# Summing the conditioning products on VectorE alone in a two-layer decoder trunk

## The chip, the cores and the metric

The kernel runs on one core of a Trainium2 chip. The metric is the device time of one execution in microseconds; lower is better. Three runs of the kernel before took 2589.61, 2590.52 and 2591.8 us.

## The reference, cut to what matters

The program is a decoder trunk of two layers on one sequence of 256 tokens, 2048 features wide, all in float32. Each layer norms its input, scales and shifts it by conditioning vectors, multiplies it with a wide input projection, mixes it in four head groups, multiplies the result with an output projection, adds it to the input through a gate, and does the same again around a gated feed-forward part. The conditioning vectors are what the change touches. They come from one vector `c` and a large matrix:

```python
cond = jax.nn.silu(c)
for l in range(DEPTH):
    mod = cond @ w_ada[l] + b_ada[l]
    shift1, scale1, gate1, shift2, scale2, gate2 = [m[:, None, :] for m in jnp.split(mod, 6, axis=-1)]
    h = rms_norm(x, norm1_w[l]) * (1.0 + scale1) + shift1
    mixed = mixer_groups(h, positions, w_in[l], ...)
    x = x + gate1 * (mixed @ w_out[l])
    h = rms_norm(x, norm2_w[l]) * (1.0 + scale2) + shift2
```

`w_ada` has 2048 rows and 12288 columns per layer, 100.7 MB. So each element of it is used once, for one product and one addition.

## The kernel before

**Dense products.** Every weight matrix is cut into pieces of 256 rows and up to 512 columns (512 KB). `prepare` loads a piece into a raw buffer from SyncE's queue (L254), ScalarE rounds it to a first float32r part `whi` (L243), and VectorE subtracts that from the raw piece to get the second part `wlo` (L246). TensorE multiplies both parts with the split activations in three products (L339 to L341, or L376 to L378). There are nine raw buffers, shared with the conditioning pieces, and four of each part; pieces are prepared three ahead. So ScalarE waits for TensorE to free a part, VectorE waits for ScalarE, and TensorE reads what both made.

**Conditioning products.** They are cut into 24 sums: in each layer four `ada_pair` sums for each of two norms (512 columns of a shift and the same 512 of a scale) and two `ada_gate` sums for each of two gates (1024 columns). One sum takes 16 units, one for each 128 rows of the matrix, so there are 384 units. A unit loads 512 KB into a raw buffer (L401 or L403). Then it goes one of two ways, by its number `k` and the tuple `on_pool`. The first unit is written into the accumulator `acc` by VectorE (L406). Units that are not in `on_pool` are multiplied and added into `acc` by one VectorE instruction (L408). Units in `on_pool` are scaled in place by ScalarE (L410) and added into a second accumulator `accb` by GpSimd (L411). `accb` is cleared by GpSimd at the first unit (L394), and the bias lands in its first partition by DMAs from GpSimd's queue (L396). `ODD` has six units (1, 3, ... 11) and serves the first four sums; `HALF` has seven (1, 3, ... 13) and serves the other twenty. That makes 164 units on GpSimd, 196 multiply-adds and 24 first units on VectorE.

**End of a sum.** After the last unit of a deferred sum, GpSimd adds `accb` to `acc` (L431 for a pair, L455 for a gate). Then TensorE sums over the partitions: for a pair by eight small matmuls with a vector of ones (L441), whose result VectorE takes over (L445, L446). The first four sums are not deferred: TensorE does eight matmuls on `accb` and then eight on `acc`, in one PSUM group. A gate's sum is split into two parts and broadcast by TensorE (L470).

**Order of the work.** The order on each engine is the order in which the Python code issues, and each engine works its queue in that order. The units wait in a queue `bg` with a due time counted in weight pieces; after each half block `pump` issues as many of them as the due times ask for, so units stand between the steps of the dense products and of the mixers on every engine. `require` issues what is left of a sum at the point where its result is needed. Accumulators are tiles of a ring of 24, which also holds activations, gates and mixer tiles.

Of the kernel before, what the change touches and what calls it, by code (L numbers as in the profile page):

```python
# [35 lines left out]
LA = 3  # L36
# [44 lines left out]
def decoder(ctx: ExitStack, tc: tile.TileContext, x_d, c_d, pos_d, w_ada, b_ada, n1_d, w_in, w2_d, b2_d,  # L81
            gnw_d, sink_d, lb_d, hnw_d, w_out, n2_d, w_fi, w_fd, fnw_d, cf_d, out_d):
    nc = tc.nc
# [6 lines left out]
    two = ctx.enter_context(tc.tile_pool(name="two", bufs=6))  # L90
# [19 lines left out]
    def MB(shape, n="m"):  # L110
        return mps.tile(shape, F32, tag="m", name=nm(n))
# [4 lines left out]
    V, A, G, TE = nc.vector, nc.scalar, nc.gpsimd, nc.tensor  # L116
# [6 lines left out]
    rows = con.tile([NROWS, P], F32, name="rows")  # L123
# [30 lines left out]
    ones = con.tile([P, 1], F32, name="ones")  # L154
# [11 lines left out]
    cond = con.tile([P, KT], F32, name="cond")  # L166
# [94 lines left out]
    def fill(n=LA):  # L261
        while len(ready) < n and (plan or cur[0] is not None):
            prepare()
# [13 lines left out]
    later = []  # L277
# [102 lines left out]
                    half()  # L380
            pump()

    # ---- conditioning vectors: products with silu(c) summed over rows on VectorE, or on ScalarE and GpSimd,
    # then over partitions on TensorE
    def ada(l, c0, pair, on_pool, finish, defer, dl):
        st = {}
        w = 512 if pair else 1024
        np_ = 1024 // w

        def unit(k):  # L390
            if k == 0:
                st["a"] = T4([P, np_, w], n="acc")
                st["b"] = T4([P, np_, w], n="accb")
                G.memset(st["b"], 0.0)  # L394
                for j in range(np_):
                    nc.gpsimd.dma_start(st["b"][0:1, j, :], b_ada[l:l + 1, c0 + j * D:c0 + j * D + w])  # L396
            raw = rawp.tile([P, np_, w], F32, tag="raw", name=nm("raw"))
            rows_ = w_ada[l, k * P:(k + 1) * P, :]
            if pair:
                src = rows_[:, c0 - c0 % D:c0 - c0 % D + 2 * D]  # L400
                nc.sync.dma_start(raw, src.rearrange("p (j n) -> p j n", j=2)[:, :, c0 % D:c0 % D + w])  # L401
            else:
                nc.sync.dma_start(raw[:, 0], rows_[:, c0:c0 + w])  # L403
            ck = cond[:, k:k + 1]
            if k == 0:
                V.tensor_scalar(out=st["a"], in0=raw, scalar1=ck, scalar2=None, op0=ALU.mult)  # L406
            elif k not in on_pool:
                V.scalar_tensor_tensor(out=st["a"], in0=raw, scalar=ck, in1=st["a"], op0=ALU.mult, op1=ALU.add)  # L408
            else:
                A.activation(raw, raw, AF.Copy, scale=ck)  # L410
                G.tensor_tensor(out=st["b"], in0=st["b"], in1=raw, op=ALU.add)  # L411
            if k == KT - 1:
                if defer is None:
                    fill()
                    finish(st["a"], st["b"])
                elif defer:
                    later.append([defer, None, lambda: finish(st["a"], st["b"])])
                else:
                    finish(st["a"], st["b"])

        for k in range(KT):
            bg.append((dl, lambda k=k: unit(k)))

    def ada_pair(l, which, g, on_pool, dl, defer=6):
        base = 0 if which == 1 else 6144
        sv, av = colv[l, "s%d" % which], colv[l, "a%d" % which]
        r = ROWS["n1" if which == 1 else "n2"] + 16 * l

        def fin(acc, accb):
            if defer:  # L430
                G.tensor_tensor(out=acc, in0=acc, in1=accb, op=ALU.add)  # L431
                later.append([3, ("c", l, which, g), lambda: reduce_(acc)])
            else:
                reduce_(accb, acc)

        def reduce_(*parts):
            ps = MB([P, 2, 4])
            for i, a in enumerate(parts):
                for j in range(2):
                    for f in range(4):  # L440
                        TE.matmul(ps[:, j, f:f + 1], a[:, j, f * P:(f + 1) * P], ones,  # L441
                                  start=i + j + f == 0, stop=i == len(parts) - 1 and j + f == 4, skip_group_check=True)
            done.add(("c", l, which, g))
            c = slice(4 * g, 4 * g + 4)
            V.tensor_copy(sv[:, c], ps[:, 0])  # L445
            V.scalar_tensor_tensor(out=av[:, c], in0=ps[:, 1], scalar=1.0, in1=cols[:, r + 4 * g:r + 4 * g + 4],  # L446
                                   op0=ALU.add, op1=ALU.mult)

        ada(l, base + 512 * g, True, on_pool, fin, defer, dl)

    gates = {}

    def ada_gate(l, which, h, on_pool, dl):
        def fin(acc, accb):
            G.tensor_tensor(out=acc, in0=acc, in1=accb, op=ALU.add)  # L455

            hls = []

            def parts():
                for j in range(2):  # L460
                    ah, al = T2([P, 512], F32R, n="ah"), T2([P, 512], F32R, n="al")
                    split(acc[:, 0, j * 512:(j + 1) * 512], ah, al, act=True)
                    hls.append((ah, al))

            def bcast():
                gt = T4([P, 1024], n="gate")
                for j in range(2):
                    ps = MB([P, 512])
                    TE.matmul(ps, ones_r, hls[j][0], start=True, stop=False)
                    TE.matmul(ps, ones_r, hls[j][1], start=False, stop=True)  # L470
                    A.activation(gt[:, j * 512:(j + 1) * 512], ps, AF.Copy)
                gates[l, which, h] = gt
                done.add(("g", l, which, h))

            later.append([2, None, parts])
            later.append([3, ("g", l, which, h), bcast])

        ada(l, (4096 if which == 1 else 10240) + h * 1024, False, on_pool, fin, 6, dl)

    # ---- norms  # L480
    ssq = con.tile([P, NT, 4], F32, name="ssq")

    def ssq_part(t, c):
# [60 lines left out]
                xs = [scaled(c + 1, t) for t in range(NT)]  # L544
            yield

    # ---- per-head norm, gate, transpose to the output projection's layout
    def to_mixed(y, mt, t):
        ps = MB([P, 4, P])
        for h in range(4):  # L550
            TE.transpose(ps[:, h], y[:, h * P:(h + 1) * P], ident)  # L551
        return lambda: split(ps, mt[0][:, :, t * P:(t + 1) * P], mt[1][:, :, t * P:(t + 1) * P], act=True)
# [645 lines left out]
        start_mix(gla_mix(l, r0, qk[:, 0:2], qk[:, 2:4], av, ag, mta))  # L1198
        return mtg, mta

    # ---- the program
    ODD = tuple(range(1, 13, 2))
    HALF = tuple(range(1, 14, 2))
    def at(W, r0, c0):
        return where[W.offset, W.shape, r0, c0]

    for g in range(4):
        ada_pair(0, 1, g, ODD, at(w_in[0], g * 512, 4368), 0 if g else None)
    for l in range(L):
        if l:  # L1210
            for g in range(4):
                ada_pair(l, 1, g, HALF, at(w_in[l], max(g - 1, 0) * 512, 5392) - (12 if g else 14))
        for h in range(2):
            ada_gate(l, 1, h, HALF, at(w_out[l], WO[3][1], 0) - 10)
        for g in range(4):
            ada_pair(l, 2, g, HALF, at(w_fi[l], max(g - 1, 0) * 512, 0) - (16 if g else 14))
        for h in range(2):
            ada_gate(l, 2, h, HALF, at(w_fd[l], 0, 0) - 6)
    def setup():
        yield from lower_bounds()  # L1220
        yield
# [61 lines left out]
    for l in range(L):  # L1283
# [50 lines left out]
        for f0, npc in PIECES:  # L1334
            ah, al = [], []
            for c in range(f0, f0 + npc):
# [44 lines left out]
                st = act_steps()  # L1381
# [12 lines left out]
            for c in range(4):  # L1394
                ps = [DB() for _ in range(NT)]
# [46 lines left out]
```

## Time and profile before

| What | Value |
|---|---|
| median of three runs | 2590.52 us |
| profiled execution: span from first to last instruction | 2585.4 us |
| profiled execution's own time | told by its span alone; the runs shown lie 4.2 to 6.4 us above it |
| TensorE busy, mean granted clock | 2444.1 us (95%), 0.979 |
| VectorE busy | 1845.5 us (71%) |
| ScalarE busy | 1268.5 us (49%) |
| GpSimd busy | 627.3 us (24%) |
| DMA: bytes, mean rate | 626.20 MB, 242 GB/s |
| L246 wlo on VectorE, 816 times | 1130.8 us |
| L411 accb on GpSimd, 164 times | 429.9 us |
| L408 acc on VectorE, 196 times | 291.0 us |
| L410 scaling on ScalarE, 164 times | 186.8 us |

Busy time is an average over stages. In the profile's view of 40 equal slices TensorE is busy nine tenths or more of almost every slice from the eleventh to the twentieth and from the thirtieth on, and less in the slices before the eleventh. A duration is the time from an instruction's start on its engine to its end, so a wait inside an instruction is counted in its duration, not as idle time.

### The profile page before, as it was taken

How to read it: one execution, taken by the hardware profiler on the slowest of the kernel's cores; microseconds unless marked ns; L12 is line 12 of the kernel's file. 1: busy time of each engine (PE TensorE's matmuls, PEld its weight loads, DVE VectorE, ACT ScalarE, POOL GpSimd, SP SyncE). 2: the span in 40 equal slices, each digit the busy share in tenths (PEclk: the TensorE clock that was granted, in tenths of full speed). 3: DMA queues.
4: the chain of work that ended last, by engine and by line, in shares of the span. 5: the costliest groups of instructions: out<-in, count | busy, mean ns of one | idle time of the engine just before them, and what ended most of it. 6: DMA issues, size and time to landing. Idle time of an engine off the chain costs nothing. (4 is left out here: it accounts for less than half of the span.)

```text
span 2585.4 us, 32744 instructions
## 1 busy us (share of the span) xinstructions
PE 2444.1 (95%) x12094; PEld 2062.7 (80%) x12094; DVE 1845.5 (71%) x1868; ACT 1268.5 (49%) x1640; POOL 627.3 (24%) x327
## 2 busy tenths in 40 slices
PE   3988788989999999999998999999999999999998
PEld 3888677867888888888877998887788888888886
DVE  7988889887777766676776786867776654555456
ACT  4535356545555454445544645555555434444444
POOL 4433455351232222221221333321132000000000
PEclk9988899999999999999999999999999999999999
DMA  8988577886988888888875857666688666666663
GB/s 288 355 283 281 157 230 234 278 291 216 315 294 283 265 292 274 274 277 277 278 251 188 277 162 247 199 221 227 214 310 288 203 193 191 187 191 192 192 205 107
DMA packets 314913, 626.20 MB, mean 242 GB/s; under 512 B 21237, under 2 KB 34401, under 8 KB 314497
## 3 DMA queue, kind: packets, MB, share of 16 engines
q1 hardware_dynamic: 312800, 622.68, 73.0%
q8 instruction: 95, 1.56, 0.2%
q10 hardware_dynamic: 528, 1.14, 0.1%
q0 software_dynamic: 1424, 0.29, 0.1%
q14 instruction: 66, 0.53, 0.1%
HBM read 621.93 MB, written 2.10 MB: 241 GB/s over the span
## 5 line engine op out<-in xcount | busy, mean ns | idle before, releaser
L246 DVE TENSOR_TENSOR wlo<-raw,whi 128x1024 fp32r<-128x1024 f32 (+2 forms) x816 | 1130.8, 1396 | 582.2 <-ACT whi L243 570.3
L243 ACT ACTIVATE whi<-raw 128x1024 fp32r<-128x1024 f32 (+2 forms) x816 | 836.2, 1033 | 780.8 <-PE d L341 637.1
L339 PE MATMUL d<-whi,hTh 128*128 128x512 f32 (+2 forms) x1888 | 738.1, 391 | 2.1 <-ACT whi L243 2.1
L340 PE MATMUL d<-wlo,hTh 128*128 128x512 f32 (+2 forms) x1888 | 726.7, 385 | 5.9 <-DVE wlo L246 5.9
L341 PE MATMUL d<-whi,hTl 128*128 128x512 f32 (+2 forms) x1888 | 726.4, 385 | 0.0
L411 POOL TENSOR_TENSOR accb<-accb,raw 128x1024 f32<-128x1024 f32 x164 | 429.9, 2621 | 1221.9 <-ACT raw L410 1145.1
L340 PEld LDWEIGHTS d<-wlo,hTh 128*128 128x128 f32 x1888 | 358.1, 190 | 74.6 <-DVE wlo L246 8.1
L341 PEld LDWEIGHTS d<-whi,hTl 128*128 128x128 f32 x1888 | 357.6, 189 | 70.7
L339 PEld LDWEIGHTS d<-whi,hTh 128*128 128x128 f32 x1888 | 358.2, 190 | 69.4 <-ACT whi L243 2.8
L408 DVE SCALAR_TENSOR_TENSOR acc<-raw,cond,acc 128x1024 f32<-128x1024 f32 x196 | 291.0, 1485 | 5.2 <-DMA raw<-in_w_ada_dram 4.9
L339 PE MATMUL d<-whi,ah 128*128 128x512 f32 x672 | 262.7, 391 | 0.0
L340 PE MATMUL d<-wlo,ah 128*128 128x512 f32 x672 | 261.6, 389 | 0.5 <-DVE wlo L246 0.5
L341 PE MATMUL d<-whi,al 128*128 128x512 f32 x672 | 261.7, 389 | 0.0
L410 ACT ACTIVATE raw<-raw,cond 128x1024 f32<-128x1024 f32 x164 | 186.8, 1139 | 9.5 <-DMA raw<-in_w_ada_dram 9.2
L340 PEld LDWEIGHTS d<-wlo,ah 128*128 128x128 f32 x672 | 126.2, 188 | 26.8 <-DVE wlo L246 0.9
L341 PEld LDWEIGHTS d<-whi,al 128*128 128x128 f32 x672 | 126.2, 188 | 26.3
L339 PEld LDWEIGHTS d<-whi,ah 128*128 128x128 f32 x672 | 126.2, 188 | 25.8
L376 PE MATMUL d<-hTh,whi 128*128 128x256 f32 x320 | 93.9, 293 | 4.4 <-DVE hTh L245 4.4
L339 PE MATMUL d<-whi,mh 128*128 128x512 f32 x224 | 90.5, 404 | 6.4 <-DVE tmp L1010 5.8
L340 PE MATMUL d<-wlo,mh 128*128 128x512 f32 x224 | 89.4, 399 | 5.6 <-DVE wlo L246 5.6
L378 PE MATMUL d<-hTl,whi 128*128 128x256 f32 x320 | 93.2, 291 | 0.7 <-DVE hTl L246 0.7
L377 PE MATMUL d<-hTh,wlo 128*128 128x256 f32 x320 | 92.8, 290 | 0.0
(293 smaller groups left out, 2509.3 us busy)
## 6 DMA issues: line engine op xcount, KB each, us to landing
raw<-in_w_ada_dram SPq DMA_DIRECT2D x384, 512.0 KB, 4.9
raw<-in_w_ffn_in_dram SPq DMA_DIRECT2D x352, 512.0 KB, 4.7
raw<-in_w_in_dram SPq DMA_DIRECT2D x176, 512.0 KB, 4.9
raw<-in_w_ffn_down_dram SPq DMA_DIRECT2D x176, 512.0 KB, 4.9
raw<-in_w_out_dram SPq DMA_DIRECT2D x64, 512.0 KB, 5.2
raw<-in_w_in_dram SPq DMA_DIRECT2D x32, 256.0 KB, 3.2
raw<-in_w_in_dram SPq DMA_DIRECT2D x16, 272.0 KB, 3.7
x<-in_x_dram SPq DMA_DIRECT2D x2, 1024.0 KB, 8.6
```

The lines of the kernel that those rows point to most:

```text
L243: A.activation(hi, src, AF.Copy)
L246: V.tensor_tensor(out=lo, in0=src, in1=hi.bitcast(F32), op=ALU.subtract)
L339: TE.matmul(o, xh, wh[:, kk], start=st, stop=False)
L340: TE.matmul(o, xh, wl[:, kk], start=False, stop=False)
L341: TE.matmul(o, xl, wh[:, kk], start=False, stop=sp)
L376: TE.matmul(o, a, hi4[:, k], start=st and f % 2 == 0, stop=False, skip_group_check=True)
L377: TE.matmul(o, b, hi4[:, k], start=False, stop=False, skip_group_check=True)
L378: TE.matmul(o, a, lo4[:, k], start=False, stop=sp and f % 2 == 1, skip_group_check=True)
L408: V.scalar_tensor_tensor(out=st["a"], in0=raw, scalar=ck, in1=st["a"], op0=ALU.mult, op1=ALU.add)
L410: A.activation(raw, raw, AF.Copy, scale=ck)
L411: G.tensor_tensor(out=st["b"], in0=st["b"], in1=raw, op=ALU.add)
```

## The change

The second accumulator, the scaling on ScalarE, the additions on GpSimd and the tuples `ODD` and `HALF` go. There is one accumulator `a` for each sum. GpSimd clears it and the bias lands in its first partition; then each of the 16 units is one multiply-add on VectorE, the first unit too. The end of a sum has no closing addition, and the first four sums reduce one accumulator by eight matmuls. Order, due times, loads and buffers stay as they are, apart from the ring of 24 tiles, from which 24 tiles fewer are drawn.

```diff
             if k == 0:
                 st["a"] = T4([P, np_, w], n="acc")
-                st["b"] = T4([P, np_, w], n="accb")
-                G.memset(st["b"], 0.0)
+                G.memset(st["a"], 0.0)
                 for j in range(np_):
-                    nc.gpsimd.dma_start(st["b"][0:1, j, :], b_ada[l:l + 1, c0 + j * D:c0 + j * D + w])
+                    nc.gpsimd.dma_start(st["a"][0:1, j, :], b_ada[l:l + 1, c0 + j * D:c0 + j * D + w])
...
-            ck = cond[:, k:k + 1]
-            if k == 0:
-                V.tensor_scalar(out=st["a"], in0=raw, scalar1=ck, scalar2=None, op0=ALU.mult)
-            elif k not in on_pool:
-                V.scalar_tensor_tensor(out=st["a"], in0=raw, scalar=ck, in1=st["a"], op0=ALU.mult, op1=ALU.add)
-            else:
-                A.activation(raw, raw, AF.Copy, scale=ck)
-                G.tensor_tensor(out=st["b"], in0=st["b"], in1=raw, op=ALU.add)
+            V.scalar_tensor_tensor(out=st["a"], in0=raw, scalar=cond[:, k:k + 1], in1=st["a"], op0=ALU.mult,
+                                   op1=ALU.add)
...
-        def fin(acc, accb):
+        def fin(acc):
             if defer:
-                G.tensor_tensor(out=acc, in0=acc, in1=accb, op=ALU.add)
                 later.append([3, ("c", l, which, g), lambda: reduce_(acc)])
             else:
-                reduce_(accb, acc)
+                reduce_(acc)
...
-            for i, a in enumerate(parts):
-                for j in range(2):
-                    for f in range(4):
-                        TE.matmul(ps[:, j, f:f + 1], a[:, j, f * P:(f + 1) * P], ones,
-                                  start=i + j + f == 0, stop=i == len(parts) - 1 and j + f == 4, skip_group_check=True)
+            for j in range(2):
+                for f in range(4):
+                    TE.matmul(ps[:, j, f:f + 1], a[:, j, f * P:(f + 1) * P], ones,
+                              start=j + f == 0, stop=j + f == 4, skip_group_check=True)
...
     def ada_gate(l, which, h, dl):
         def fin(acc):
-            G.tensor_tensor(out=acc, in0=acc, in1=accb, op=ALU.add)
```

## Rows read from the trace of the kernel before

**Rows 1.** Busy time by stretch: PE, PEld, DVE, ACT, POOL, clock, DMA share, GB/s.
```profile
48.40:257.00 208.60, 188.10 (x1149) 171.78 (x1149) 186.52 (x171) 105.73 (x128) 83.56 (x38) 0.92 0.87 298
257.00:646.00 389.00, 344.90 (x1758) 289.74 (x1757) 329.23 (x379) 198.24 (x326) 163.49 (x87) 0.93 0.71 235
646.00:1292.00 646.00, 644.72 (x2912) 534.03 (x2911) 462.23 (x384) 324.81 (x340) 164.00 (x77) 1.00 0.84 283
1292.00:1874.00 582.00, 556.88 (x3114) 479.30 (x3113) 426.17 (x506) 304.06 (x466) 154.12 (x87) 0.99 0.68 221
```
**Rows 2.** Waits from 48.4 to 257: who for whom, us, times, longest.
```profile
DVE s L445 <- PE m L441: 13.5, 4, 5.4
...
PE m L376 <- DVE hv L1138: 8.3, 3, 4.0
```
**Rows 3.** Groups by form, VectorE, from 2068 on: busy us, mean ns, idle before.
```profile
L246 DVE TENSOR_TENSOR wlo<-raw,whi 128x1024 fp32r<-128x1024 f32 x181 | 220.2, 1225 | 209.5 <-ACT whi L243 207.7 <-DMA raw<-in_w_ffn_in_dram 1.7
```
**Rows 4.** The same view from 48.4 to 257.
```profile
L246 DVE TENSOR_TENSOR wlo<-raw,whi 128x1024 fp32r<-128x1024 f32 x45 | 82.3, 1843 | 4.7 <-ACT whi L243 4.7
L408 DVE SCALAR_TENSOR_TENSOR acc<-raw,cond,acc 128x1024 f32<-128x1024 f32 x35 | 55.2, 1579 | 0.1
L498 DVE TENSOR_SCALAR xs<-x,rstd 128x512 f32<-128x512 f32 x6 | 10.2, 1735 | 0.0
```
**Rows 5.** One line's instructions over the span: ns min/median/max, first and last start.
```profile
L408 DVE SCALAR_TENSOR_TENSOR acc<-raw,cond,acc x196: 1260/1278/3467, 14.4 to 2003.8; 128x1024 f32<-128x1024 f32 x196
...
L406 DVE TENSOR_SCALAR acc<-raw,cond x24: 739/748/2889, 8.7 to 1927.0; 128x1024 f32<-128x1024 f32 x24
```
**Rows 6.** Timeline of VectorE and of GpSimd from 160: start us, duration us.
```profile
160.81 4.55 DVE L246 TENSOR_TENSOR wlo<-raw,whi 128x1024 fp32r<-128x1024 f32 x2
...
159.69 3.45 POOL L411 TENSOR_TENSOR accb<-accb,raw 128x1024 f32<-128x1024 f32 x1 [3.94 <-ACT raw L410]
```
**Rows 7.** Groups by form, VectorE, from 0 to 48.4.
```profile
L408 DVE SCALAR_TENSOR_TENSOR acc<-raw,cond,acc 128x1024 f32<-128x1024 f32 x9 | 17.8, 1979 | 5.0 <-DMA raw<-in_w_ada_dram 4.9
...
L213 DVE TENSOR_SCALAR kk<-kk 128x128 f32<-128x128 f32 x1 | 2.4, 2378 | 0.0
...
L498 DVE TENSOR_SCALAR xs<-x,rstd 128x512 f32<-128x512 f32 x2 | 1.0, 488 | 0.1
```
**Rows 8.** GpSimd's additions L411 by stretch: busy us and count.
```profile
48.40:257.00 208.60, 73.74 (x25) 0.92 0.87 298
257.00:646.00 389.00, 97.09 (x37) 0.93 0.71 235
646.00:1292.00 646.00, 128.80 (x52) 1.00 0.84 283
1292.00:1874.00 582.00, 85.31 (x33) 0.99 0.68 221
```
**Rows 9.** Timeline of TensorE: one reduction's matmuls on accb, then on acc.
```profile
142.38 1.84 PE L441 MATMUL m<-ones,accb 128*128 128x1 f32 x16
144.08 1.93 PE L441 MATMUL m<-ones,acc 128*128 128x1 f32 x16
```
**Rows 10.** Groups by form, VectorE, from 257 to 646.
```profile
L246 DVE TENSOR_TENSOR wlo<-raw,whi 128x1024 fp32r<-128x1024 f32 x84 | 133.9, 1603 | 33.0 <-ACT whi L243 32.6
L408 DVE SCALAR_TENSOR_TENSOR acc<-raw,cond,acc 128x1024 f32<-128x1024 f32 x41 | 69.0, 1682 | 0.0
```
**Rows 11.** Groups by form, VectorE, from 646 to 1292.
```profile
L246 DVE TENSOR_TENSOR wlo<-raw,whi 128x1024 fp32r<-128x1024 f32 x232 | 336.1, 1457 | 163.0 <-ACT whi L243 162.3
```
**Rows 12.** Groups by form, VectorE, from 1292 to 1874.
```profile
L246 DVE TENSOR_TENSOR wlo<-raw,whi 128x1024 fp32r<-128x1024 f32 x155 | 218.9, 1425 | 86.0 <-ACT whi L243 81.6 <-DMA raw<-in_w_ada_dram 3.5 <-DMA raw<-in_w_ffn_in_dram 0.3
```
**Rows 13.** Timelines from 1570, then the bias DMA's landing (us min/median/max).
```profile
1571.42 0.95 POOL L394 MEMSET accb<- 128x1024 f32 x1
1572.67 1.03 POOL L396 DMA_DIRECT2D accb<-in_b_ada_dram x2 [0.29 <-POOL accb L394]
...
1574.70 0.75 DVE L406 TENSOR_SCALAR acc<-raw,cond 128x1024 f32<-128x1024 f32 x1
...
DMA to landing us min/median/max: 1.7/4.7/6.0
```

More of the change, by code (lines that the diff above doesn't have):

```diff
@@ L381, in block_T, with ada @@
             pump()
-    def ada(l, c0, pair, on_pool, finish, defer, dl):
+    def ada(l, c0, pair, finish, defer, dl):
         st = {}
@@ L414, in unit, with ada_pair @@
                     fill()
-                    finish(st["a"], st["b"])
+                    finish(st["a"])
                 elif defer:
-                    later.append([defer, None, lambda: finish(st["a"], st["b"])])
+                    later.append([defer, None, lambda: finish(st["a"])])
                 else:
-                    finish(st["a"], st["b"])
+                    finish(st["a"])
         for k in range(KT):
             bg.append((dl, lambda k=k: unit(k)))
-    def ada_pair(l, which, g, on_pool, dl, defer=6):
+    def ada_pair(l, which, g, dl, defer=6):
         base = 0 if which == 1 else 6144
@@ L427, in ada_pair, with reduce_ @@
         r = ROWS["n1" if which == 1 else "n2"] + 16 * l
-        def fin(acc, accb):
+        def fin(acc):
             if defer:
-                G.tensor_tensor(out=acc, in0=acc, in1=accb, op=ALU.add)
                 later.append([3, ("c", l, which, g), lambda: reduce_(acc)])
             else:
-                reduce_(accb, acc)
-        def reduce_(*parts):
+                reduce_(acc)
+        def reduce_(a):
             ps = MB([P, 2, 4])
-            for i, a in enumerate(parts):
-                for j in range(2):
-                    for f in range(4):
-                        TE.matmul(ps[:, j, f:f + 1], a[:, j, f * P:(f + 1) * P], ones,
-                                  start=i + j + f == 0, stop=i == len(parts) - 1 and j + f == 4, skip_group_check=True)
+            for j in range(2):
+                for f in range(4):
+                    TE.matmul(ps[:, j, f:f + 1], a[:, j, f * P:(f + 1) * P], ones,
+                              start=j + f == 0, stop=j + f == 4, skip_group_check=True)
             done.add(("c", l, which, g))
@@ L447, in reduce_, with ada_gate, fin @@
                                    op0=ALU.add, op1=ALU.mult)
-        ada(l, base + 512 * g, True, on_pool, fin, defer, dl)
+        ada(l, base + 512 * g, True, fin, defer, dl)
     gates = {}
-    def ada_gate(l, which, h, on_pool, dl):
-        def fin(acc, accb):
-            G.tensor_tensor(out=acc, in0=acc, in1=accb, op=ALU.add)
+    def ada_gate(l, which, h, dl):
+        def fin(acc):
             hls = []
@@ L476, in fin @@
             later.append([3, ("g", l, which, h), bcast])
-        ada(l, (4096 if which == 1 else 10240) + h * 1024, False, on_pool, fin, 6, dl)
+        ada(l, (4096 if which == 1 else 10240) + h * 1024, False, fin, 6, dl)
     ssq = con.tile([P, NT, 4], F32, name="ssq")
@@ L1199, in first_groups @@
         return mtg, mta
-    ODD = tuple(range(1, 13, 2))
-    HALF = tuple(range(1, 14, 2))
     def at(W, r0, c0):
@@ L1207, in decoder @@
     for g in range(4):
-        ada_pair(0, 1, g, ODD, at(w_in[0], g * 512, 4368), 0 if g else None)
+        ada_pair(0, 1, g, at(w_in[0], g * 512, 4368), 0 if g else None)
     for l in range(L):
@@ L1211, in decoder @@
             for g in range(4):
-                ada_pair(l, 1, g, HALF, at(w_in[l], max(g - 1, 0) * 512, 5392) - (12 if g else 14))
+                ada_pair(l, 1, g, at(w_in[l], max(g - 1, 0) * 512, 5392) - (12 if g else 14))
         for h in range(2):
-            ada_gate(l, 1, h, HALF, at(w_out[l], WO[3][1], 0) - 10)
+            ada_gate(l, 1, h, at(w_out[l], WO[3][1], 0) - 10)
         for g in range(4):
-            ada_pair(l, 2, g, HALF, at(w_fi[l], max(g - 1, 0) * 512, 0) - (16 if g else 14))
+            ada_pair(l, 2, g, at(w_fi[l], max(g - 1, 0) * 512, 0) - (16 if g else 14))
         for h in range(2):
-            ada_gate(l, 2, h, HALF, at(w_fd[l], 0, 0) - 6)
+            ada_gate(l, 2, h, at(w_fd[l], 0, 0) - 6)
     def setup():
```

## The prediction

> **What bounds the kernel now.** I read the page's span first (2585.4 us, in the table of times), then the busy table over stretches that I cut where the code changes its work [rows 1]: start (to 48.4), the four input groups of layer 0 (48.4 to 257), the mixers and output projection of layer 0 (257 to 646), the feed-forward part of layer 0 (646 to 1292), the same mixers of layer 1 (1292 to 1874); what follows has little or no conditioning work. The reader is to see two regimes. From 646 to 1292 TensorE is busy 644.7 of 646.0 us at a granted clock of 1.00 (its level of 2.4 GHz), VectorE only 462.2: the products set the pace. From 48.4 to 257 VectorE is busy 186.5 of 208.6 us, while TensorE has 20.5 us idle and a mean granted clock of 0.92, so part of the stretch at the lower level; from 257 to 646 VectorE is busy 329.2 of 389.0, TensorE idle 44.1 at 0.93. There VectorE is the engine that others wait for: the waits name it ahead of TensorE (hv, 8.3 us in three waits, [rows 2]), and what it waits for itself is the small reduction on TensorE (13.5 us in four waits, same group).
>
> Why VectorE is so full stands in its durations. With no conditioning work about, the subtraction that makes wlo takes 1225 ns [rows 3]; from 48.4 to 257 it takes 1843 ns on average [rows 4]. The multiply-add on the accumulator takes 1260 ns at best and 3467 at worst, 1278 in the middle [rows 5]. One place shows the cause: GpSimd's addition starts at 159.69 and lasts 3.45 us, and the two subtractions beside it take 4.55 us instead of 2 x 1.225 = 2.45 [rows 6]. So an addition on GpSimd costs VectorE about 2.1 us there, more than the 1.28 us that VectorE would need to do the addition itself.
>
> **The change part by part.** In all, 164 scalings on ScalarE and 164 additions on GpSimd become 164 multiply-adds of 1.28 us on VectorE, 210 us; 24 first pieces become multiply-adds too (1.28 for 0.75, [rows 5], 24 x 0.53 = 13 us). Against these 223 us stands what VectorE's other work loses in length. I take it stage by stage, give-back = count x (mean - clean duration), and ask how much lies on the path.
>
> Start. Give-back: 9 multiply-adds x (1.979 - 1.278) = 6.3 us, and the stretched L213 of 2.38 us, which by the larger xs operation (0.49 us) should be under 0.5, so 1.9, and L212 alike: 10 us [rows 7]. New: 6 pieces (1, 3, ... 11) x 1.28 + 0.53 = 8.2. Net -1.8; VectorE works through its queue here until the reduction can start, so I take -2 (bounds -4 and +2).
>
> Input groups. Give-back: wlo 45 x 0.618 = 27.8, multiply-add 35 x 0.301 = 10.5, xs 6 x (1.735 - 0.488) = 7.5, together 45.8 us [rows 4]. New: 25 additions [rows 8] x 1.28 + 5 x 0.53 = 34.7. Net -11.1 of VectorE. Beside it three reductions lose their first half: the matmuls on accb take 1.84 us [rows 9], of which 1.70 pass before those on acc start, and VectorE waits for their end: 3 x 1.7 = 5.1. Of -16.2 I take -14, because VectorE is busy 89% here. Bounds: 0, if TensorE and the transfers are late instead, and -28, if all 20.5 us of TensorE's idle time and half of its lost clock (0.08 x 188 / 2 = 7.5) come back.
>
> Mixers of layer 0. Give-back in two forms: wlo 84 x 0.378 = 31.8, multiply-add 41 x 0.404 = 16.6, so 48.4 [rows 10]; other forms are stretched too, but GpSimd's mixer products, which stay, share in that. Equal in size to the new 37 x 1.28 + 5 x 0.53 = 50.1 [rows 8]. The other forms decide: were the rest of VectorE's work (329 - 134 - 69 = 126 us) stretched by only a tenth, that is 12 us more. I take -8 (bounds +2 and -25). The closing additions acc<-acc,accb on GpSimd go as well; they are in these means.
>
> Feed-forward of layer 0. Give-back in wlo alone 232 x (1.457 - 1.225) = 54 us [rows 11]; new 52 x 1.28 + 7 x 0.53 = 70 [rows 8]. VectorE gets 16 us longer and no time moves: 184 us of VectorE's idle time in that stretch [rows 1] hide it. Without that cover it would cost the 16.
>
> Mixers of layer 1. Give-back in wlo 155 x 0.200 = 31 us [rows 12]; new 33 x 1.28 + 5 x 0.53 = 44.9 [rows 8]. That is +14, less what the multiply-adds and other forms give back. VectorE is busy 73% and TensorE 96%: I take 0 (+5 to -8). ScalarE's 164 scalings went beside other work: its wait is for TensorE, so I cost their end at nothing.
>
> The new wait. VectorE's first multiply-add now reads the accumulator, so it waits for memset (0.95 us), two DMA issues on GpSimd's queue and the landing of the bias. Queued behind it on VectorE is the next wlo, and for that TensorE. Price of one, if fully exposed: 0.95 + 0.29 + 1.03 + a landing of 4.7 in the middle = 7.0 us [rows 13]. In the case shown memset starts at 1571.42, so the bias would be there at about 1578.4, and VectorE came to its first piece at 1574.70: 3.7 us late. That is the latest I find of 24; mostly VectorE comes well after the landing, and GpSimd, with no additions ahead of the memset, will be earlier than now. Loads, memsets and bias DMAs stay the same in number and order. Raw buffers come free at the end of the multiply-add, not of GpSimd's addition, so loads go out no later. I take +2 (bounds 0 and 24 x 7.0 = 168).
>
> The clock is in no term so far: the stretches in which TensorE idles are those with a lower granted clock [rows 1]; if it idles less I expect more of the upper level, an estimate of which I count -4 (a tenth of 0.08 x 188 + 0.07 x 345 = 39 us).
>
> Sum: -2 - 14 - 8 + 0 + 0 + 2 - 4 = -26, so a span of 2559.4 us. The median of the runs is 5.1 us above the span, for what lies around it: 2564.
>
> On the lock there is a figure to set beside: the Trainium skill, SBUF — State Buffer, section SBUF: two separate sides, says that a VectorE operation with two SBUF inputs and a GpSimd operation that reads SBUF hold one port pair in turn, each for its whole length. The stretched rows agree in kind. By that rule the 25 additions of the input groups could give back up to their whole 25 x 2.4 = 60 us, not 45.8, and the stage -25; I keep the rows' figure.
>
> **The rivals.**
> More comes back than I count: TensorE's idle time before 646 (20.5 + 44.1) shrinks by half and its clock with it (20 of 39 us). For it: VectorE is what it waits for. Against it: serial mixer steps cause part of the idling. -52 and the -2 of the start: 2536.
>
> The saving is hidden: in the input groups ScalarE waits for TensorE and for transfers already, and TensorE is busy 90% at the low clock. VectorE then only idles more: -3, 2588.
>
> Slower, by an overfull VectorE: the stretched durations don't come from GpSimd's additions but from the crowd of other traffic in those stages, and don't come back. Then the input groups need 186.5 + 34.7 = 221 us of VectorE where 208.6 are, +13 plus its 13.5 us of waits, and the mixers 329 + 50 = 379 of 389, with waits some +20: +45, 2635. It decides from the point where less than 35 of the 45.8 us come back. Against it: rows 3 and 6. The Trainium skill, Perfetto Trace Analysis, section Optimizing Scalar/DVE Operations, is on its side in part: it holds moving work off a saturated VectorE to ScalarE or even GpSimd to make sense, and warns in the same place that the shared port can spoil it. No row of this trace shows the first half at work.
>
> Slower, by the bias: should more than four or five first pieces in VectorE-bound stages stand the full 7.0 us, the gain is gone; with ten, 2564 + 70 = 2634. Against it: the one late case above.
>
> **How the numbers follow.** My forecast (-12 to -45) 0.55; more back 0.13; hidden (-12 to +5) 0.19; overfull VectorE 0.08; bias 0.05. A difference under 0.2%, 5.2 us, can't be told from none. Faster by more: 0.55 + 0.13 + 0.08 of the hidden cases = 0.76; same 0.11; slower 0.13. The range from 2535 to 2590 takes in the forecast, the hidden cases up to no change and most of the first rival, and leaves out some 0.2.
>
> **What would show it.** In the changed profile wlo from 48 to 257 should take under 1.35 us and the multiply-add 1.28 with 384 of them; VectorE's busy time over the span should be about the same, within 60 us of 1845, with GpSimd under 200. The input groups should end near 240, and the feed-forward part should take 646 us as now. Wrong would be: wlo still at 1.6 us or more without GpSimd; a row of VectorE waiting for the bias DMA for over 10 us in sum; or TensorE as idle as before with VectorE idle beside it.

## The result and the profile after

The changed kernel takes 2509.3 us (median of four runs, 2508.65 to 2511.46); the kernel before took 2591.0 beside it. The ratio is 0.969, with a 95% interval from 0.9675 to 0.9706: 3.1% faster, 82 us, where 26 were forecast, and below the range's lower end of 2535. The direction was right, the size wrong by a factor of three.

The span fell from 2585.4 to 2507.8 us. I cut both traces at the same points of the program, found by the number of the weight piece that ScalarE rounds:

| Stage | before, us | after, us | change | forecast |
|---|---|---|---|---|
| start | 48.4 | 44.4 | -4.0 | -2 |
| input groups, layer 0 | 208.6 | 189.0 | -19.6 | -14 |
| mixers and output projection, layer 0 | 389.0 | 351.6 | -37.4 | -8 |
| feed-forward, layer 0 | 646.0 | 645.2 | -0.8 | 0 |
| mixers and output projection, layer 1 | 582.0 | 566.3 | -15.7 | 0 |
| rest | 711.4 | 711.3 | -0.1 | 0 |

(The forecast had -4 for the clock and +2 for the bias besides, without a stage.) In the runs on record a time lies 1.7 to 2.3 us above its own span, so the profiled execution of the kernel before was some 3 us shorter than the median run: the stages add up to 77.6 us, not to 82.

First the busy table by stretch after the change, as in [rows 1]: PE, PEld, DVE, ACT, POOL with counts, granted clock, DMA share, GB/s.

```profile
44.40:233.40 189.00, 176.34 (x1106) 160.19 (x1105) 171.36 (x198) 79.53 (x103) 8.09 (x10) 0.95 0.95 331
233.40:585.00 351.60, 329.66 (x1749) 277.65 (x1748) 304.94 (x415) 159.97 (x288) 53.12 (x52) 0.98 0.77 259
585.00:1230.20 645.20, 645.20 (x2917) 535.16 (x2916) 466.77 (x436) 272.72 (x289) 9.57 (x14) 1.00 0.83 284
1230.20:1796.50 566.30, 551.42 (x3114) 477.04 (x3113) 423.36 (x540) 270.36 (x432) 51.92 (x47) 0.99 0.69 226
```

Three things are to be seen. VectorE has 36 instructions more in the mixers of layer 0 (415 for 379), and is busy 24 us less (304.9 for 329.2). TensorE is idle 21.9 us there where it was 44.1, and does nearly the same matmuls (1749 for 1758) in 15 us less, at a mean granted clock of 0.98 for 0.93, so with more of the stretch at the level of 2.4 GHz. And the feed-forward part did not move: TensorE filled it before and fills it now.

The groups by form on VectorE show where the time came from. The first two lines are of 44.4 to 233.4 (answering [rows 4]), then one each of 233.4 to 585 ([rows 10]), 585 to 1230 ([rows 11]) and 1230 to 1797 ([rows 12]). The columns after the bar: busy us and mean ns of one, then the idle time before them and what ended it.

```profile
L403 DVE SCALAR_TENSOR_TENSOR acc<-raw,cond,acc 128x1024 f32<-128x1024 f32 x65 | 83.1, 1278 | 0.3
L246 DVE TENSOR_TENSOR wlo<-raw,whi 128x1024 fp32r<-128x1024 f32 x46 | 56.5, 1231 | 4.1 <-ACT whi L243 4.0
...
L246 DVE TENSOR_TENSOR wlo<-raw,whi 128x1024 fp32r<-128x1024 f32 x83 | 101.1, 1223 | 21.2 <-ACT whi L243 20.6 <-DMA raw<-in_w_ffn_in_dram 0.3
...
L246 DVE TENSOR_TENSOR wlo<-raw,whi 128x1024 fp32r<-128x1024 f32 x232 | 282.2, 1223 | 152.8 <-ACT whi L243 143.3 <-DMA raw<-in_w_ffn_in_dram 9.4
...
L246 DVE TENSOR_TENSOR wlo<-raw,whi 128x1024 fp32r<-128x1024 f32 x156 | 191.8, 1240 | 79.5 <-ACT whi L243 77.1 <-DMA raw<-in_w_out_dram 1.8
```

The subtraction that makes wlo takes 1.22 to 1.24 us in each of these stages, its clean duration of [rows 3]; it took 1.84, 1.60, 1.46 and 1.43 before. On the timeline after, where [rows 6] showed two subtractions of 4.55 us together, subtraction and multiply-add follow each other at full pace:

```profile
146.49 1.22 DVE L246 TENSOR_TENSOR wlo<-raw,whi 128x1024 fp32r<-128x1024 f32 x1
147.63 1.28 DVE L403 SCALAR_TENSOR_TENSOR acc<-raw,cond,acc 128x1024 f32<-128x1024 f32 x1
148.82 1.22 DVE L246 TENSOR_TENSOR wlo<-raw,whi 128x1024 fp32r<-128x1024 f32 x1
149.96 1.28 DVE L403 SCALAR_TENSOR_TENSOR acc<-raw,cond,acc 128x1024 f32<-128x1024 f32 x1
```

The page's busy lines sum it up: 384 multiply-adds in place of 220 first pieces and multiply-adds, and still 42.5 us less than the 1845.5 of before on VectorE.

```profile
PE 2408.2 (96%) x12030; PEld 2034.0 (81%) x12030; DVE 1803.0 (72%) x2032; ACT 1100.7 (44%) x1476; POOL 133.9 (5%) x143
```

The new wait hardly exists. The multiply-add's own view, over the whole span, names what ended VectorE's idle time before it, with us and times; the 7.3 us are the very first piece, which waited 7.0 us for another reason before. The landing of a bias held VectorE up a single time, for 1.4 us, against the +2 that I had taken for this wait.

```profile
L403 DVE SCALAR_TENSOR_TENSOR acc<-raw,cond,acc x384: 1266/1278/2533, 9.1 to 1926.2; 128x1024 f32<-128x1024 f32 x192
...
  POOL acc L393: 7.3, 1
  DMA raw<-in_w_ada_dram: 3.5, 2
  DMA acc<-in_b_ada_dram: 1.4, 1
```

### The profile page after: what moved, and what is told of

Same layout as the page of the kernel before. It is cut to its first block, busy times and chain, and to the rows that moved or that the text cites. A ratio compares the mean times of both kernels' runs of the same rounds, so it can differ in the third digit from the quotient of the medians.

```text
span 2507.8 us, 32376 instructions
## 1 busy us (share of the span) xinstructions
PE 2408.2 (96%) x12030; PEld 2034.0 (81%) x12030; DVE 1803.0 (72%) x2032; ACT 1100.7 (44%) x1476; POOL 133.9 (5%) x143
## 5 line engine op out<-in xcount | busy, mean ns | idle before, releaser
L246 DVE TENSOR_TENSOR wlo<-raw,whi 128x1024 fp32r<-128x1024 f32 (+2 forms) x816 | 970.7, 1197 | 547.9 <-ACT whi L243 526.8
L403 DVE SCALAR_TENSOR_TENSOR acc<-raw,cond,acc 128x1024 f32<-128x1024 f32 x384 | 500.5, 1304 | 13.1 <-POOL acc L393 7.3
L341 PE MATMUL d<-whi,ml 128*128 128x512 f32 x224 | 87.8, 392 | 0.0
L339 PE MATMUL m<-whi,hTh 128*128 128x512 f32 (+2 forms) x184 | 68.5, 372 | 6.3 <-DVE hg L1127 4.7
```

The lines of the kernel that those rows point to most:

```text
L339: TE.matmul(o, xh, wh[:, kk], start=st, stop=False)
L341: TE.matmul(o, xl, wh[:, kk], start=False, stop=sp)
L403: V.scalar_tensor_tensor(out=st["a"], in0=raw, scalar=cond[:, k:k + 1], in1=st["a"], op0=ALU.mult, op1=ALU.add)
```

## The experiments

The theory: an addition on GpSimd reads SBUF and stalls VectorE's two-input operations, and that is most of the loss. Rivals: GpSimd's additions filled its own queue and kept raw buffers occupied; ScalarE's scalings made whi late; the second accumulator with its closing additions cost the time.

**Additions on GpSimd, put back beside the change.** The units stay on VectorE; behind 164 of them GpSimd adds the used raw piece to itself.

```diff
             V.scalar_tensor_tensor(out=st["a"], in0=raw, scalar=cond[:, k:k + 1], in1=st["a"], op0=ALU.mult,
                                    op1=ALU.add)
+            if k % 2 and k < (13 if l == 0 and c0 < 2048 else 14):
+                G.tensor_tensor(out=raw, in0=raw, in1=raw, op=ALU.add)
```

> The changed kernel, and behind the VectorE multiply-add of each of the 164 units that GpSimd took before, GpSimd adds the used raw piece to itself; nobody reads that sum. VectorE's own work is that of the changed kernel (2509.3 us). Theory (an addition on GpSimd that reads SBUF stalls VectorE's two-input operations): wlo beside them goes from 1.23 back to 1.6 us or more in the stages before the feed-forward part, VectorE's busy time grows by 150 us or more, and the time goes to 2600 to 2690 us, above the kernel before, since VectorE now does the sums as well. Rival queue (the mixers' own steps on GpSimd stood behind the additions): wlo stays at 1.23 us, time 2530 to 2570, the same as in the memset kernel. Rival buffers (raw pieces came free later): the same as the memset kernel too.

Measured: 2613.0 us, ratio 1.0086 (1.0067 to 1.0105): 104 us above the changed kernel and above the kernel before.

**The same place in GpSimd's queue without a read.**

```diff
-                G.tensor_tensor(out=raw, in0=raw, in1=raw, op=ALU.add)
+                r2 = raw.rearrange("p j n -> p (j n)")
+                G.memset(r2, 0.0)
+                G.memset(r2, 1.0)
+                G.memset(r2[:, 0:512], 0.0)
```

> As the kernel with the additions, but in their place GpSimd clears the used raw piece two and a half times, about 2.4 us as an addition takes alone: the same place in GpSimd's queue, the same hold on the raw buffer, but no read of SBUF. Theory: wlo stays at 1.23 us, time 2505 to 2520. Rivals queue and buffers: as slow as the kernel with the additions, 2530 to 2570.

Measured: 2539.4 us, ratio 0.9802 (0.9785 to 0.9819), 30 us above the changed kernel. Here are the input groups of the two, first of the kernel with additions: its busy time by stretch, then two groups of VectorE there.

```profile
52.10:275.30 223.20, 188.31 (x1104) 168.96 (x1103) 208.19 (x196) 79.29 (x103) 70.09 (x38) 0.89 0.84 280
```

```profile
L403 DVE SCALAR_TENSOR_TENSOR acc<-raw,cond,acc 128x1024 f32<-128x1024 f32 x65 | 104.4, 1606 | 1.0 <-issue 0.7
L246 DVE TENSOR_TENSOR wlo<-raw,whi 128x1024 fp32r<-128x1024 f32 x45 | 65.2, 1450 | 2.3 <-ACT whi L243 2.3
```

The same two views of the kernel that clears:

```profile
45.20:243.40 198.20, 177.97 (x1110) 161.25 (x1111) 179.99 (x199) 79.49 (x103) 71.96 (x88) 0.95 0.94 323
```

```profile
L403 DVE SCALAR_TENSOR_TENSOR acc<-raw,cond,acc 128x1024 f32<-128x1024 f32 x65 | 84.2, 1296 | 1.5 <-issue 0.9 <-DMA raw<-in_w_ada_dram 0.2
L246 DVE TENSOR_TENSOR wlo<-raw,whi 128x1024 fp32r<-128x1024 f32 x46 | 56.2, 1225 | 5.2 <-ACT whi L243 5.1
```

GpSimd is busy 70 and 72 us in both, and its instructions stand at the same places behind the same units. With a read wlo takes 1450 ns, without one 1225. So the stall of these two-input operations hangs on the read of SBUF, not on GpSimd being at work; 74 of the 104 us go with it. The Trainium skill, SBUF — State Buffer, section SBUF: two separate sides, says that a VectorE operation with two SBUF inputs contends with GpSimd only where GpSimd's operation reads SBUF; these two runs agree. The theory's number for the second kernel, 2505 to 2520, was missed: 30 us stay. A part of them is VectorE's own. Operations with one large input are stretched by the clearing as well, as this one over the whole span, first in the kernel that clears, then in the changed kernel:

```profile
L1069 DVE TENSOR_SCALAR hf<-hf,omt,lbt 128x256 f32<-128x256 f32 x8 | 6.6, 865 | 0.0
L1064 DVE TENSOR_SCALAR hf<-hf,omt,lbt 128x256 f32<-128x256 f32 x8 | 2.9, 407 | 0.0
```

In the input groups VectorE is busy 180.0 us where the changed kernel has 171.4, and the stage is 9.2 us longer. The rest is left to the rivals. The waits of the clearing kernel over the whole span show two pieces of it:

```profile
ACT whi L243 <- DMA raw<-in_w_in_dram: 36.9, 23, 3.0
ACT whi L243 <- DMA raw<-in_w_out_dram: 17.9, 10, 4.3
...
DVE acc L403 <- DMA acc<-in_b_ada_dram: 13.7, 5, 5.0
```

In the changed kernel the same three are 17.1, 11.1 and 1.4 us. So raw buffers that come free later make ScalarE wait for loads, and a busy GpSimd makes the bias late. These are waits, not all of them on the path. In the kernel before the two waits of ScalarE are 16.0 and 0.4 us, no more than in the changed kernel: there GpSimd's addition took the place of VectorE's step on a raw buffer, here the clearing comes behind it. So the 30 us are not shown to be a cost of the kernel before.

**ScalarE's scalings put back.**

```diff
+            if k % 2 and k < (13 if l == 0 and c0 < 2048 else 14):
+                A.activation(spare, raw.rearrange("p j n -> p (j n)"), AF.Copy, scale=cond[:, k:k + 1])
             V.scalar_tensor_tensor(out=st["a"], in0=raw, scalar=cond[:, k:k + 1], in1=st["a"], op0=ALU.mult,
```

> The changed kernel, with the 164 scalings on ScalarE put back ahead of the multiply-add, into a spare tile (bfloat16) that nobody reads. Theory: ScalarE had idle time beside them (780 us before whi alone), time 2507 to 2520. Rival (ScalarE's scalings made whi late): 2530 to 2570.

Measured: 2517.1 us, ratio 0.9716 (0.9696 to 0.9736): 8 us, within the theory's range, though the intervals of this ratio and of the change's overlap.

**The kernel before with empty tuples.**

```diff
-    ODD = tuple(range(1, 13, 2))
-    HALF = tuple(range(1, 14, 2))
+    ODD = ()
+    HALF = ()
```

> The kernel before with empty tuples: no unit goes to ScalarE and GpSimd, but the second accumulator, its clearing, the bias in it, the closing additions on GpSimd, the ring of 24 tiles and the first units without a read of the accumulator stay. Theory: only 20 of 184 additions are left, so 2505 to 2525 us. Rival (the single accumulator and its bias order, and fewer tiles drawn from the ring, make the gain): it stays near 2570 to 2600.

Measured: 2528.2 us, ratio 0.9758 (0.974 to 0.9775): a little above what the theory said, 64 us below the kernel before beside it and 19 above the changed kernel. So the gain comes apart in two steps: some 64 us for the units that went to VectorE, and 19 for the second accumulator with its 20 closing additions.

**Three units of each sum on GpSimd** (the same edit with the tuples (3, 7, 11)).

> The kernel before with three units of each sum on ScalarE and GpSimd (3, 7, 11) in place of six or seven: 72 additions, where it had 164 and the kernel with empty tuples none (2528 us). Theory (each addition costs its stall): about in proportion, 2545 to 2568 us. Rival (GpSimd must be loaded above some point before it harms): within 5 us of 2528.

Measured: 2550.6 us, ratio 0.9844 (0.9825 to 0.9864), inside the theory's range. From 0 to 72 additions the time grows by 22 us (0.31 each), from 72 to 164 by some 42 (0.45 each): about in proportion, somewhat steeper at the end, and no threshold.

**The mixers' own steps moved to VectorE as well.**

```diff
-                G.tensor_tensor(out=sl_, in0=sl_, in1=pr[:, :, B - 1:B].to_broadcast([P, n, B]), op=ALU.mult)
+                V.tensor_tensor(out=sl_, in0=sl_, in1=pr[:, :, B - 1:B].to_broadcast([P, n, B]), op=ALU.mult)
...
-        G.tensor_tensor(out=dst[:, :, 0:n], in0=dst[:, :, 0:n], in1=tmp, op=ALU.add)
+        V.tensor_tensor(out=dst[:, :, 0:n], in0=dst[:, :, 0:n], in1=tmp, op=ALU.add)
```

(and the gates' products and a copy likewise)

> The changed kernel with the mixers' own products and additions on GpSimd (some 60 instructions, 134 us of GpSimd with the clearing) moved to VectorE too, so that only clearing and bias loads are left on GpSimd. Theory: what they stall comes back and pays for their time on VectorE, and the steps of the mixers' chains get shorter: 2495 to 2510. Rival (VectorE is full in the mixers, and a product on GpSimd beside it is free): 2512 to 2525.

Measured: 2518.7 us, ratio 0.9721 (0.9701 to 0.9742): the rival was right, the theory's number wrong, though the intervals of this ratio and of the change's touch here too. These steps on GpSimd do stretch VectorE (the longest multiply-add of the changed kernel is 2533 ns, of this one 1286), but as work on VectorE they cost more. The same stretch of the program, first in the changed kernel, then in this one: VectorE goes from 313.0 to 320.3 us busy, and the stretch from 362.0 to 367.7.

```profile
235.40:597.40 362.00, 340.06 (x1789) 286.17 (x1789) 312.95 (x419) 165.50 (x294) 53.12 (x52) 0.98 0.77 261
```

```profile
235.90:603.60 367.70, 340.14 (x1790) 285.71 (x1789) 320.28 (x445) 165.48 (x295) 17.50 (x26) 0.98 0.76 257
```

**The kernel before without the reads.**

```diff
                 A.activation(raw, raw, AF.Copy, scale=ck)
-                G.tensor_tensor(out=st["b"], in0=st["b"], in1=raw, op=ALU.add)
+                r2 = raw.rearrange("p j n -> p (j n)")
+                G.memset(r2, 0.0)
+                G.memset(r2, 1.0)
+                G.memset(r2[:, 0:512], 0.0)
```

> The kernel before, with each of GpSimd's 164 additions replaced by clearing the scaled raw piece two and a half times (about 2.4 us), so that 164 of the 384 units are left out of the sums; scaling on ScalarE, GpSimd's queue, the hold on raw buffers, the closing additions and VectorE's work stay. Theory (the read of SBUF on GpSimd is what costs): wlo at 1.23 us outside the closing additions and 2500 to 2535 us, although VectorE still does only 220 of the units. Rival (the queue of GpSimd and the raw buffers that it holds): 2565 to 2595.

Measured: 2521.7 us, ratio 0.973 (0.9713 to 0.9747): 71 us gone where only the reading additions were replaced. Its input groups (busy by stretch, then two groups of VectorE):

```profile
45.00:239.20 194.20, 185.83 (x1151) 171.35 (x1149) 145.08 (x169) 105.29 (x128) 71.89 (x88) 0.93 0.91 320
```

```profile
L246 DVE TENSOR_TENSOR wlo<-raw,whi 128x1024 fp32r<-128x1024 f32 x45 | 55.1, 1228 | 24.3 <-ACT whi L243 24.2
...
L501 DVE TENSOR_SCALAR xs<-x,rstd 128x512 f32<-128x512 f32 x6 | 6.2, 1080 | 0.0
```

VectorE falls from 186.5 to 145.1 us with the same instructions as before, so 41 us of stalls, near the 45.8 that the prediction read from the durations; most of the difference is xs, an operation with one large input, which at 1080 ns is still over twice as long as its 488 of [rows 7]. The stage gets 14 us shorter, not 41. VectorE now waits 24 us for whi: another limit is next.

**More raw buffers, a smaller ring** (NRAW 9 to 11, NBIG 24 to 22).

> The changed kernel with 11 raw buffers in place of 9 and a ring of 22 tiles in place of 24. If the time that raw buffers are held was a part of the loss (and is still one): 2485 to 2503 us, with ScalarE's waits for weight loads gone. If not: 2506 to 2513; slower if the smaller ring makes clearing the accumulators wait.

Measured: 2515.6 us, ratio 0.9706 (0.9689 to 0.9723), not to be told from the changed kernel's 0.969. More raw buffers don't make the changed kernel faster, at least not beside a smaller ring, which the same run has: ScalarE's waits for pieces of w_in, 17.1 us in the changed kernel, are 17.5 here. On the kernel before it says nothing.

**The same additions on VectorE instead of GpSimd.**

```diff
+            if k % 2 and k < (13 if l == 0 and c0 < 2048 else 14):
+                V.scalar_tensor_tensor(out=raw, in0=raw, scalar=2.0, in1=raw, op0=ALU.mult, op1=ALU.add)
```

> The changed kernel, and behind the multiply-add of each of the 164 units that GpSimd took before, a second multiply-add of the same size on VectorE over the used raw piece, which nobody reads: 164 x 1.28 = 210 us more of VectorE's work, no GpSimd. It measures what the prediction priced at full length, 1.28 us on the path for each addition in the stages before the feed-forward part. If that price is right: the input groups 25 to 32 us longer, the mixers of layer 0 some 40 and those of layer 1 some 20, so 2590 us or more. If VectorE's own work mostly lies beside other work (the lesson from the kernel without reads, 2521.7 with 223 us less on VectorE than the changed kernel): 2515 to 2555, and in any case under the 2613 of the kernel with as many additions on GpSimd.

Measured: 2588.0 us, ratio 0.9988 (0.9977 to 0.9999). The 210 us of VectorE work cost 79 us; it holds the raw buffers longer, too. That falls between what was expected: nearer to the prediction's price than to my idea, after the kernel without reads, that VectorE's own work lies mostly beside other work. That idea fell. The input groups, the mixers of layer 0 and, with some pieces of the feed-forward part, those of layer 1 (busy by stretch):

```profile
49.00:264.80 215.80, 185.29 (x1106) 166.41 (x1106) 200.70 (x222) 79.44 (x103) 8.38 (x10) 0.92 0.87 290
267.00:654.20 387.20, 343.37 (x1740) 285.74 (x1740) 347.26 (x448) 159.92 (x289) 52.80 (x52) 0.94 0.71 234
1291.60:1906.00 614.40, 591.87 (x3275) 507.73 (x3274) 494.82 (x601) 287.41 (x450) 52.53 (x48) 0.99 0.70 227
```

The added line in the three stretches (by form in the first and the third, by stretch in the second):

```profile
L406 DVE SCALAR_TENSOR_TENSOR raw<-raw 128x1024 f32<-128x1024 f32 x25 | 30.6, 1225 | 0.9
...
267.00:654.20 387.20, 44.44 (x37) 0.94 0.71 234
...
L406 DVE SCALAR_TENSOR_TENSOR raw<-raw 128x1024 f32<-128x1024 f32 x37 | 46.7, 1263 | 1.3
```

And the second and third stretch, between the same pieces, in the changed kernel:

```profile
235.40:586.10 350.70, 328.76 (x1740) 276.80 (x1740) 304.04 (x412) 159.97 (x288) 53.12 (x52) 0.98 0.76 259
1223.20:1825.40 602.20, 587.32 (x3276) 506.75 (x3275) 451.08 (x565) 287.40 (x450) 52.88 (x48) 0.99 0.70 232
```

30.6 us of added work make this stage 26.8 us longer (215.8 for 189.0), so 88% of it: here VectorE is the limit. In the mixers of layer 0, 44.4 us of it cost 36.5 (387.2 for 350.7), 82%. In those of layer 1, 46.7 us of it cost 12.2 (614.4 for 602.2), a quarter. Against the kernel with the additions on GpSimd the comparison is direct: the same 164 additions beside the same work cost 104 us on GpSimd and 79 on VectorE.

**The tables of sines and cosines worked out later.**

```diff
-        if k >= 2:
+        if 2 <= k < 7:
             next(prep, None)
...
+    for i in range(6):
+        later.append([6 + 2 * i, None, lambda: next(prep, None)])
```

> The changed kernel with the tables of sines and cosines worked out after the first reduction instead of between the first conditioning pieces. In the changed kernel VectorE ends the first sum at 40.9 us, some 9 us after its last piece has landed, with 4.6 us of these tables in its queue before. If VectorE's queue sets the start there: the first products 3 to 5 us earlier and 2503 to 2508 us. If the loads set it: no change, 2507 to 2512.

Measured: 2508.0 us, ratio 0.9682 (0.9667 to 0.9697). The first sum is taken over by VectorE at 41.1 us instead of 44.7, as VectorE's queue would have it, but the span is only 0.4 us shorter: the lead is given back in the following stages. It is not shown to be faster than the changed kernel.

**The closing additions on VectorE, in the kernel before.**

```diff
-                G.tensor_tensor(out=acc, in0=acc, in1=accb, op=ALU.add)
+                V.tensor_tensor(out=acc, in0=acc, in1=accb, op=ALU.add)
```

(in both places)

> The kernel before with its 20 closing additions (acc <- acc, accb, 2.4 to 5.6 us each on GpSimd) moved to VectorE; all else stays. The reversals so far, taken one at a time from the changed kernel, add up to about 52 of the 82 us, so some 30 are not accounted for. If the closing additions, which come where a sum is about to be needed, cost more in the full kernel than the 19 us between the kernel with empty tuples and the changed one: 2560 to 2572 us. If they cost about that: 2572 to 2582. If the 19 us came from the second accumulator otherwise: 2585 to 2593.

Measured: 2577.9 us beside 2590.5, ratio 0.9951 (0.9936 to 0.9966): 13 us, in the middle range. These additions take 1.2 to 1.4 us on VectorE, and took 3.1 to 3.5 us on GpSimd.

```profile
L431 DVE TENSOR_TENSOR acc<-acc,accb 128x1024 f32<-128x1024 f32 x12 | 16.8, 1401 | 0.0
L455 DVE TENSOR_TENSOR acc<-acc,accb 128x1024 f32<-128x1024 f32 x8 | 9.7, 1217 | 0.0
```

**No scaling on ScalarE, in the kernel before.**

```diff
-                A.activation(raw, raw, AF.Copy, scale=ck)
                 G.tensor_tensor(out=st["b"], in0=st["b"], in1=raw, op=ALU.add)
```

> The kernel before without the 164 scalings on ScalarE: GpSimd adds the raw piece unscaled, so the scaling of these units is left out of the computation; its queue, its reads and VectorE's work stay. If ScalarE's part is the 8 us that the scalings cost when put back into the changed kernel: 2580 to 2588. If it is more beside GpSimd's additions (VectorE waits for whi behind a scaling, and GpSimd for the scaling): 2560 to 2578. If nothing, as predicted: 2588 to 2594.

Measured: 2580.2 us, ratio 0.9957 (0.9941 to 0.9974): 10 us. The scalings were not free.

## Why the prediction was wrong

**Right: the mechanism and the place.** GpSimd's additions stall VectorE, as read from [rows 4 to 6]. The kernel before without the reads takes 71 us less, and a clearing at the same place leaves wlo at its clean length. The input groups and the mixers of layer 0 moved, as named, the feed-forward part kept its length, and the bias wait was 1.4 us. The mixers of layer 1 moved too, against a forecast of 0.

**Right in size: the give-back where I read it by forms.** In the input groups 45.8 us of stalls were read from the durations; without the reads VectorE's busy time fell there by 41, and not by the 60 that whole additions would give. There the forecast of -14 met -19.6. Nor was the price of a multiply-add far off there: 88% of it lay on the path in the input groups, about the share that I used (14 of 16.2).

**Wrong: the mixers, -8 and 0 where -37 and -16 were measured.** Here are the four stages in five of the kernels, in us, cut where ScalarE starts to round the same weight pieces, from the fourth to the 567th (so the lengths differ by up to 2 us from the table above):

| Stage | before | no reads | empty tuples | changed | doubled |
|---|---|---|---|---|---|
| input groups, layer 0 | 207.0 | 193.1 | 192.0 | 188.0 | 214.7 |
| mixers and output projection, layer 0 | 386.8 | 349.0 | 361.8 | 350.7 | 387.2 |
| feed-forward, layer 0 | 647.2 | 645.5 | 645.3 | 645.3 | 645.5 |
| mixers and output projection, layer 1 | 581.7 | 573.7 | 570.6 | 565.9 | 578.2 |

From "before" to "empty tuples" the units go to VectorE, from there to "changed" the second accumulator goes. In the input groups the two steps are -15.0 and -4.0, where the prediction had -11.1 and -5.1. In the mixers they are -25.0 and -11.1 in layer 0, -11.1 and -4.7 in layer 1, where it had -8 and 0 for the first and nothing for the second. Three steps failed there.
- I counted the give-back in two forms, put a tenth on the rest, 12 us, and then took the balance of VectorE's busy time for the gain. In the mixers of layer 0 the rest gave back some 26 us: without wlo, the multiply-adds and the first pieces, VectorE was busy some 120 us before and 95 after. These lines, of 257 to 646 before and of 233.4 to 585 after, belong to that sum; hf is one of the stretched rest.

```profile
L666 DVE TENSOR_TENSOR hf<-hf 128x512 f32<-128x512 f32 x7 | 9.1, 1304 | 3.0 <-POOL Sx L665 3.0
L406 DVE TENSOR_SCALAR acc<-raw,cond 128x1024 f32<-128x1024 f32 x5 | 5.9, 1174 | 0.0
...
L403 DVE SCALAR_TENSOR_TENSOR acc<-raw,cond,acc 128x1024 f32<-128x1024 f32 x83 | 109.1, 1315 | 0.4
L655 DVE TENSOR_TENSOR hf<-hf 128x512 f32<-128x512 f32 x7 | 4.8, 687 | 2.6 <-POOL Sx L654 2.6
```

  So VectorE's busy time fell by 24 us there, three times what I took; the price was not what failed, for 82% of the doubled work lies on the path. In the mixers of layer 1 busy time fell by 3, near my 0, and yet 16 us came off: there the balance of busy time is no measure. Of the doubled work on VectorE a quarter is on the path there, against 88% in the input groups, so VectorE's busy time says little on the length of that stage; what made its -11.1 is open.
- I costed three things at nothing. Two were not nothing. ScalarE's scalings ("its wait is for TensorE, so I cost their end at nothing"): 10 us in the kernel before, 8 when put back. The closing additions ("they are in these means"): 13 us when moved, and 19 between the kernel with empty tuples and the changed one, the second accumulator included, of which the prediction had 5.1 in the input groups. For GpSimd's queue and the hold on raw buffers ("so loads go out no later") the kernel that clears sets an upper bound of 30 us, and the waits of the kernel before show little sign of it.
- The clock had -4. TensorE's busy time fell by 36 us over the span (2444.1 to 2408.2), of which 9 are the 64 matmul records on accb that are gone; the other 27 go with a mean granted clock of 0.95 and 0.98 for 0.92 and 0.93 in the first two stages. Over the whole span the means of 0.979 and 0.990 come to some 109 us at the level of 1.2 GHz before and 50 after. In the input groups TensorE is idle 20.5 us before, at 0.92 [rows 1], and 12.7 after, at 0.95; with the additions put back 34.9, at 0.89. But the kernel before without the reads has 0.93 at only 8.4 us idle, so idle time alone doesn't tell it, and no run here changed the clock alone: its share of the gain, up to those 27 us, stays an estimate.

A smaller slip: the median was put 5.1 us above the span, of which some 2 lie around every span and 3 were the one profiled execution's.

**How it adds up, and what stays open.** The parts do not add up to the whole. Taken from the kernel before one at a time, the reads are worth 71 us, closing additions 13 and scalings 10, together 94, and the price of the 164 units has to come off. By the doubled units it is 79 us, on a VectorE that already had all 384; then 15 of the 82 us are explained, 45 with the full 30 of queue and buffers. For 82 to come out the price would have to be 12 us, or 42 with those 30; neither was measured by itself. Put back into the changed kernel one at a time, additions on GpSimd in place of VectorE (104 - 79), scalings (8) and the second accumulator (19) make 52. So some 30 us or more belong to no part alone: the parts lean on each other, and the clock, which is in each of them, may be why. That is not shown.

**The rivals.** "More comes back" was the case, at 0.13, and even its 2536 fell short. Its condition held: TensorE's idle time in the first two of these stages fell from 64.6 to 34.6 us, about by half. Its against was serial mixer steps; some of these were stretched themselves, such as hf above, 1304 ns before and 687 after. The overfull VectorE was refuted by wlo at 1.23 us, the hidden saving by the input groups' 19.6 us, and the bias by its 1.4 us. The Trainium skill, Perfetto Trace Analysis, section Optimizing Scalar/DVE Operations, says that moving work off a saturated VectorE can make sense, with a warning of the shared port; for these 164 units the warning held. The mixers' own steps, which are few, seem better on GpSimd (2518.7 with them on VectorE). The range was too narrow in the mixers: its bounds there were -25 and -8, and -37.4 and -15.7 were measured.

## What to carry to other kernels

Where two engines stretch each other's instructions, compare an instruction's duration in a stretch without the neighbour with its duration beside it, over all forms, before crediting an idle engine with free work. Busy time saved is not the gain: 41 us of it on VectorE gave 14 in one stage here, and 3 gave 16 in another, so price everything that a change removes, closing steps and scalings on other engines too, and do not expect the prices to add up. A pair of runs that keeps the queue and the timing and takes away only one property of an instruction, as the clearing for the addition here, tells a stall from a busy queue.

## What the hardware showed that was not expected

Clearing SBUF on GpSimd, 2.4 us at a time, left VectorE's operations at 1225 ns, while additions of 2410 ns on the mean took them to 1450 at the same places: for these two-input operations being busy is no contention, reading is. Operations with one large input are stretched by clearing too (hf at 865 ns for 407). And the price of 1.28 us more on VectorE was 0.48 us of the kernel's time on the mean (79 us / 164), that of an addition on GpSimd 0.63 (104 us / 164), though VectorE was at 72% and GpSimd at 5% of the span.
